# Moving the last two thirds of an adaLN modulation from VectorE to quarter-array matmuls on TensorE, in a one-core hybrid encoder layer

## The chip, the core and the metric

The kernel runs on one core of one Trainium2 chip. The metric is the device time of one execution in microseconds (us), the median of three runs. Engines are named as in the profile: PE is TensorE (PEld its weight loads), DVE is VectorE, ACT is ScalarE, POOL is GpSimd, SP is the queue from which all DMAs are issued.

## What is computed

One encoder layer over a prompt of 512 frames and a sample of 64 frames, all in float32. The change concerns the modulation vector `mod`: two conditioning vectors of 2048 elements (prompt and sample) pass through silu and a 2048 x 12288 matrix, and the result is cut into six shift, scale and gate vectors.

```
def trunk(x, c, states, params, block):
    ...
        mod = jax.nn.silu(c) @ w_ada[l] + b_ada[l]
        sh1, sc1, g1, sh2, sc2, g2 = jnp.split(mod[:, None, :], N_MOD, axis=-1)
        h = rmsnorm(x, norm1[l]) * (1 + sc1) + sh1
        mix, s_a, s_b, s_c = token_mixers(
        ...
        x = x + g1 * mix
        h = rmsnorm(x, norm2[l]) * (1 + sc2) + sh2
        f, s_f = conv_ffn(h, ffn_s[l], w_up[l], ffn_conv_w[l], ffn_conv_b[l], w_down[l])
        x = x + g2 * f
```

The mixers are a gated linear attention of 4 heads and a gated DeltaNet of 8 heads, evaluated in blocks of 64 or 128 frames between a wide input projection and an output projection. A convolutional FFN follows.

## The kernel before, in words

Large products run on PE as three float32r matmuls for each 128 x 128 weight tile and half of the frames (288 columns): high part times high part, high times low, low times high (`mm6`, L512 and L514). ACT and DVE split each weight tile into its parts ahead of time (`split`, L599 and L600).

**Stages.** `head` (to about 165 us of the span) norms the input and computes shift 1 and scale 1, that is columns 0 to 4095 of `w_ada`. The mixing stage (to about 1260 us) computes the input projection tile by tile and, woven into it, the recurrences. Then come the second half of the output projection, the FFN's upward products, and its downward products.

**The modulation in the head** (`modulation`, L659) goes by PE: for 512 columns and four k-tiles of 128 rows, four matmuls (L672) run, each with a stationary tile of 32 columns of which two hold the conditioning vectors (`cs`), each writing its own 32 partitions of one PSUM bank. The four quarters are summed at the end by a transposition on PE (L144) and a reduction on DVE (L678).

**The modulation in the mixing stage** (`ada_block`, L757) goes by DVE: columns 4096 to 12287, 16 blocks of 512. For each block, DVE multiplies each of 16 k-tiles (128 x 512) by a column of the conditioning vector and adds it to an accumulator, for both vectors: 32 instructions (L770 for the first k-tile, L772 for the others). Then eight PE matmuls of one column (L778) sum over the partitions, and DVE adds the bias (L747). The weights come in loads of two k-tiles, 512 KB each (L764), into a pool of two buffers with the tag `xr`; the same two buffers serve the reloads of the input in the output projection (`x_tile`, L1093) and some reloads of mixer outputs.

**What sets the order.** The mixing stage is one stream of `mm6` calls; after each (one k-tile, six matmuls) `tick` (L479) advances the recurrences' generators by one step and the modulation's generator by 0.65 steps. A `yield` ends a step, and `rest(n)` lets n steps pass with nothing. A scheduler then fixes the order of each engine's instructions before the program runs; every engine's queue, SP's too, is worked in that order.

**The inverse.** Each DeltaNet head needs the inverse of 16 x 16 triangular blocks (`inverse16`, L331). It goes: PE L216 (products of keys), DVE, a store by SP (L340) and four loads (L345), some 30 small steps on POOL (L347 to L354), a store (L355) and two loads (L358), and two DVE instructions (L362) that spread the result. There are nine of these: eight prompt heads, here h0 to h7, and the sample. While one head's inverse is on its way, the steps of the head before run on PE: L276, L283, L289, L301 to L305 four times over, then a norm (DVE L137, POOL L138, ACT) and a transposition on PE (L144).

Of the kernel before, what the change touches and what calls it, by code (L numbers as in the profile page):

```python
# [16 lines left out]
P = 128  # L17
# [78 lines left out]
class Kern:  # L96
# [510 lines left out]
    def head(self, pool):  # L607
# [8 lines left out]
        nc.gpsimd.memset(cs, 0.0)  # L616
        for s in range(2):
            A.activation(self.ct[:, s], self.vmap[f"c{s}"], AF.Silu)
            V.tensor_copy(cs[:, :, s], self.ct[:, s])
        self.mod = self.cp.tile([P, 6, KD, 2], F32, name="mod")  # L620


# [36 lines left out]
        def modulation(g):  # L659
            for mi in (1, 0):  # L660
                ps = self.bank()
                c0 = mi * D + g * 512
                for k0 in range(0, KD, 4):
                    yield
                    raws = [hraw().rearrange("p (k n) -> p k n", k=2) for _ in range(2)]
                    for n, raw in enumerate(raws):
                        k1 = k0 + 2 * n
                        nc.sync.dma_start(raw, i["w_ada"][0, k1 * P:(k1 + 2) * P, c0:c0 + 512].rearrange("(k p) n -> p k n", p=P))

                    for k in (2, 3, 0, 1):  # L670
                        with self.tc.issue_after(last) if k == 0 else nullcontext():
                            T.matmul(ps[32 * k:32 * k + 32], cs[:, k0 + k], raws[k // 2][:, k % 2], start=(k0 == 0), stop=(k0 == KD - 4))  # L672
                        last = nc.cur_bb.bb.instructions[-1]
                rw = pool.tile([P, 512], F32, tag="rw", bufs=1, name=self.name("rw"))
                V.tensor_copy(rw, ps)
                pc = self.transpose4(rw.rearrange("p (b t) -> p b t", b=4))
                m = pool.tile([P, 4, 2], F32, tag="msum", bufs=2, name=self.name("msum"))
                V.tensor_reduce(m, pc.rearrange("p b (j q) -> p b q j", j=4)[:, :, 0:2], axis=mybir.AxisListType.X, op=ALU.add)  # L678
# [12 lines left out]
        for g in range(4):  # L691
# [22 lines left out]
                next(mods, None)  # L714
            for _ in mods:
                pass

    def pair_w(self, offs, k0):

# [34 lines left out]
            out[:, k0:k0 + n], self.mod[:, mi, k0:k0 + n], 1.0,  # L754
            self.vec(norm, k0, n).unsqueeze(2).to_broadcast([P, n, 2]), op0=ALU.add, op1=ALU.mult)

    def ada_block(self, blk, acc, raw):  # L757

        nc = self.nc
        V, T = nc.vector, nc.tensor  # L760
        acc = [a() for a in acc]
        for k0 in range(0, KD, 2):
            w = raw().rearrange("p (k n) -> p k n", k=2)
            nc.sync.dma_start(w, self.i["w_ada"][0, k0 * P:(k0 + 2) * P, blk * 512:(blk + 1) * 512]  # L764
                              .rearrange("(k p) n -> p k n", p=P))
            for k in range(2):
                for s in range(2):
                    col = self.ct[:, s, k0 + k:k0 + k + 1]
                    if k0 + k == 0:
                        V.tensor_scalar_mul(acc[s], w[:, k], col)  # L770
                    else:
                        V.scalar_tensor_tensor(acc[s], w[:, k], col, acc[s], op0=ALU.mult, op1=ALU.add)  # L772
                    yield
        yield from self.rest(4)
        pc = self.bank()
        for j in range(4):
            for s in range(2):
                T.matmul(pc[:, 2 * j + s:2 * j + s + 1], acc[s][:, j * P:(j + 1) * P], self.c["ones"][:, 0:1],  # L778
                         start=True, stop=True)
        self.put_mod(blk // 4, 4 * (blk % 4), pc[:, :8].rearrange("p (j s) -> p j s", s=2))  # L780

    def ada_blocks(self, blocks, acc):
        for blk in blocks:
            yield from self.ada_block(blk, acc, self.xr)


    def w_in(self, off):
# [746 lines left out]
def layer_kernel(tc, i, o):  # L1534
    nc = tc.nc
    with ExitStack() as ctx:
# [16 lines left out]
        with ExitStack() as early:  # L1553
            K.wp = pool(early, "wp", "right", bufs=3)
            with ExitStack() as right:
# [9 lines left out]
                with ExitStack() as st:  # L1565
                    K.ap = pool(st, "ap", bufs=1)
                    K.jobs, K.at_job, K.at_ada = [], 0.0, 0.0
                    K.dp = dp
                    acc = [lambda n=n: K.ap.tile([P, 512], F32, tag=f"acc{n}", bufs=1, name=K.name("acc")) for n in range(2)]
# [12 lines left out]
                    for _ in K.ada:  # L1582
                        pass
# [101 lines left out]
```

## Time and profile before

| | |
|---|---|
| median of three runs | 2984.51 us (2979.99 to 2984.74) |
| the profiled execution | 2981.26 us, span 2979.5 us |
| mean granted TensorE clock | 0.980 |
| PE, DVE, ACT, POOL busy | 96%, 69%, 40%, 11% of the span |
| PE without work in 200 to 1260 us | 66 us |
| DVE in L772 | 480 instructions, 340.5 us |
| DVE in L770 | 32 instructions, 14.7 us |
| moved by DMA | 395.55 MB, mean 133 GB/s |

How to read the rows in the prediction: a row of the timeline has the start, the duration (of a run of like instructions, from the first start to the last end), the engine, the line of the program, the operation, out<-in, the count, and in brackets how long the engine was idle before and what ended the wait. PE's rows overlap, since matmuls are pipelined: what one costs in the stream is read from one start to the next. A float32 matmul shows as two records, a float32r matmul as one. A row of stretches has the length of the stretch, the busy time of each engine with its instruction count, the granted clock (1.00 is full speed), and the busy share and GB/s of the DMA engines.

### The profile page before, as it was taken

To read this page: it belongs to the slowest core of one execution; us is meant where nothing else is said; L and a number is where in the kernel's file an instruction comes from. 1 tells how busy PE (TensorE), PEld (TensorE's weight loads), DVE (VectorE), ACT (ScalarE), POOL (GpSimd) and SP (SyncE) were. 2 spreads that over 40 slices of the span, in tenths; PEclk is the share of its full clock that TensorE was granted. 3 is DMA by queue.
4 is the path that set the end of the run, shared out by engine and by line. 5 is a ranking of instruction groups with operands and counts; after the bars stand their busy time and mean duration, and the time that the engine had idled before them with its cause. 6 is when DMAs were issued, how large, how long until landed. Compare 5 with 4: busy or idle time off the path is not lost.

```text
span 2979.5 us, 52341 instructions
## 1 busy us (share of the span) xinstructions
PE 2863.4 (96%) x21060; PEld 2772.9 (93%) x21060; DVE 2050.0 (69%) x3234; ACT 1179.3 (40%) x2015; POOL 338.0 (11%) x609
## 2 busy tenths in 40 slices
PE   6998899999899999999999999999999999999998
PEld 3688888999889998999999999999999999999997
DVE  2366766667668867557888888888888865555555
ACT  4234444444445333245444444444444421222223
POOL 0004323333120000000011111111111100000000
PEclk8999999999999999999999999999999999999999
DMA  8864544444454446643333333333333473333221
GB/s 269 285 185 121 150 143 124 128 129 144 134 159 130 137 132 194 199 140 97 106 105 111 109 103 107 111 102 105 115 105 105 133 236 101 111 101 113 84 85 66
DMA packets 535446, 395.55 MB, mean 133 GB/s; under 512 B 59657, under 2 KB 465412, under 8 KB 535204
## 3 DMA queue, kind: packets, MB, share of 16 engines
q1 hardware_dynamic: 535204, 392.21, 44.0%
q8 instruction: 166, 2.72, 0.4%
q14 instruction: 76, 0.62, 0.1%
HBM read 356.47 MB, written 35.67 MB: 132 GB/s over the span
## 4 chain that ended last, share of the span: by engine, by line
PE 71%; DVE 3%; DMA 2%; POOL 1%; issue 1%; ACT 1%; SPq 0%; ACTq 0%; DVEq 0%; POOLq 0%
PE g L512 22%; PE bank L1301 11%; PE bank L1300 11%; PE bank L1302 11%; PE g L514 11%; DVE acc L772 1%; PE bank L405 1%; PE bank L144 1%; DMA xr<-in_w_ada_dram 1%; DMA xr<-in_x_prompt_dram 1%; PE bank L778 1%; DVE wl L600 0%; POOL m L352 0%; POOL m L351 0%; POOL s L138 0%
## 5 line engine op out<-in xcount | busy, mean ns | idle before, releaser
L1301 PE MATMUL bank<-slot,wh 128*128 128x290 f32 x2464 | 736.3, 299 | 0.0
L1300 PE MATMUL bank<-slot,wh 128*128 128x290 f32 x2464 | 734.0, 298 | 0.0
L1302 PE MATMUL bank<-slot,wl 128*128 128x290 f32 x2464 | 728.2, 296 | 0.0
L512 PE MATMUL g<-slot,wh 128*128 128x288 f32 x3168 | 551.7, 295 | 0.3 <-DVE slot L1070 0.3
L512 PE MATMUL g<-hh,wh 128*128 128x288 f32 x2048 | 473.1, 310 | 0.0
L1302 PEld LDWEIGHTS bank<-slot,wl 128*128 128x128 f32 x2464 | 470.8, 191 | 0.0
L1301 PEld LDWEIGHTS bank<-slot,wh 128*128 128x128 f32 x2464 | 469.8, 191 | 0.1
L512 PEld LDWEIGHTS g<-slot,wh 128*128 128x128 f32 x3168 | 465.8, 188 | 0.7 <-DVE slot L1070 0.5
L599 ACT ACTIVATE wh<-raw 128x1024 fp32r<-128x1024 f32 x215 | 227.5, 1059 | 601.9 <-PE g L512 572.1
L1300 PEld LDWEIGHTS bank<-slot,wh 128*128 128x128 f32 x2464 | 464.2, 188 | 0.1
L512 PE MATMUL g<-hl,wh 128*128 128x288 f32 x2048 | 461.6, 304 | 0.0
L514 PE MATMUL g<-hh,wl 128*128 128x288 f32 x2048 | 459.9, 303 | 1.6 <-DVE wl L600 1.6
L1070 DVE SCALAR_TENSOR_TENSOR slot<-g,mod,slot 128x512 f32<-128x512 f32 (+1 forms) x448 | 202.1, 492 | 284.2 <-PE g L514 283.2
L772 DVE SCALAR_TENSOR_TENSOR acc<-xr,ct,acc 128x512 f32<-128x512 f32 x480 | 340.5, 752 | 26.6 <-DMA xr<-in_w_ada_dram 26.0
L512 PEld LDWEIGHTS g<-hh,wh 128*128 128x128 f32 x2048 | 336.6, 193 | 12.1 <-issue 9.8
L514 PEld LDWEIGHTS g<-hh,wl 128*128 128x128 f32 x2048 | 338.6, 193 | 8.4 <-issue 5.9
L512 PEld LDWEIGHTS g<-hl,wh 128*128 128x128 f32 x2048 | 340.4, 193 | 4.4 <-issue 3.9
L514 PE MATMUL g<-slot,wl 128*128 128x288 f32 x1584 | 342.8, 295 | 0.0
L600 DVE TENSOR_TENSOR wl<-raw,wh 128x1024 fp32r<-128x1024 f32 x215 | 262.5, 1221 | 62.4 <-ACT wh L599 61.7
L1247 ACT ACTIVATE wh<-raw 128x1024 fp32r<-128x1024 f32 x176 | 186.0, 1057 | 221.9 <-PE bank L1301 185.6
L514 PEld LDWEIGHTS g<-slot,wl 128*128 128x128 f32 x1584 | 255.3, 188 | 0.0
L1248 DVE TENSOR_TENSOR wl<-raw,wh 128x1024 fp32r<-128x1024 f32 x176 | 215.4, 1224 | 54.3 <-ACT wh L1247 54.3
(354 smaller groups left out, 3160.9 us busy)
## 6 DMA issues: line engine op xcount, KB each, us to landing
raw<-in_w_up_dram SPq DMA_DIRECT2D x176, 512.0 KB
xr<-in_w_ada_dram SPq DMA_DIRECT2D x128, 512.0 KB
raw<-in_w_in_dram SPq DMA_DIRECT2D x100, 512.0 KB
raw<-in_w_down_dram SPq DMA_DIRECT2D x88, 512.0 KB
hraw<-in_w_ada_dram SPq DMA_DIRECT2D x64, 512.0 KB
raw<-in_w_out_dram SPq DMA_DIRECT2D x32, 512.0 KB
slot<-actd SPq DMA_DIRECT2D x44, 288.0 KB
actd<-v SPq DMA_DIRECT2D x44, 256.0 KB
```

Of the source, the lines that this page charges most:

```text
L144: self.nc.tensor.transpose(ps[:, b * P:(b + 1) * P], src4[:, b], self.c["ident"])
L512: T.matmul(ps[:, h if bank is None else bank, :n], wh, x[:, h, :n], start=f, stop=False)
L514: T.matmul(ps[:, h if bank is None else bank, :n], wl, ah[:, h, :n], start=False, stop=stop)
L599: nc.scalar.activation(hi[:, :n_], raw[:, :n_], AF.Copy)
L600: nc.vector.tensor_tensor(lo[:, :n_], raw[:, :n_], hi[:, :n_].bitcast(F32), op=ALU.subtract)
L772: V.scalar_tensor_tensor(acc[s], w[:, k], col, acc[s], op0=ALU.mult, op1=ALU.add)
L1070: self.nc.vector.scalar_tensor_tensor(x1[:, :, z], ps[:, :, c], gain[:, q:q + 1], x1[:, :, z], op0=ALU.mult, op1=ALU.add)
L1247: self.nc.scalar.activation(hi, src, AF.Copy)
L1248: self.nc.vector.tensor_tensor(lo, src, hi.bitcast(F32), op=ALU.subtract)
L1300: T.matmul(ps, wh[:, j], hi, start=(c < 3 and j == 0), stop=False, skip_group_check=True)
L1301: T.matmul(ps, wh[:, j], lo, start=False, stop=False, skip_group_check=True)
L1302: T.matmul(ps, wl[:, j], hi, start=False, stop=(j == NPAIR - 1), skip_group_check=True)
```

## The change

All 16 blocks of the mixing stage are now computed in the manner of the head, with one difference: each group of four matmuls is a sum of its own (start and stop both set), and DVE adds it from PSUM to one accumulator in SBUF. The head's code is moved into helpers that both places call (`c_columns`, `quad`, `load_ada`, `quad_sum`); what it issues stays the same.

```
-    def ada_block(self, blk, acc, raw):
...
-        acc = [a() for a in acc]
-        for k0 in range(0, KD, 2):
-            w = raw().rearrange("p (k n) -> p k n", k=2)
-            nc.sync.dma_start(w, self.i["w_ada"][0, k0 * P:(k0 + 2) * P, blk * 512:(blk + 1) * 512]
-                              .rearrange("(k p) n -> p k n", p=P))
-            for k in range(2):
-                for s in range(2):
-                    col = self.ct[:, s, k0 + k:k0 + k + 1]
-                    if k0 + k == 0:
-                        V.tensor_scalar_mul(acc[s], w[:, k], col)
-                    else:
-                        V.scalar_tensor_tensor(acc[s], w[:, k], col, acc[s], op0=ALU.mult, op1=ALU.add)
-                    yield
-        yield from self.rest(4)
-        pc = self.bank()
-        for j in range(4):
-            for s in range(2):
-                T.matmul(pc[:, 2 * j + s:2 * j + s + 1], acc[s][:, j * P:(j + 1) * P], self.c["ones"][:, 0:1],
-                         start=True, stop=True)
-        self.put_mod(blk // 4, 4 * (blk % 4), pc[:, :8].rearrange("p (j s) -> p j s", s=2))
+    def quad(self, ps, c, raws, start, stop):
+
+        for k in (2, 3, 0, 1):
+            with self.tc.issue_after(last) if k == 0 else nullcontext():
+                self.nc.tensor.matmul(ps[32 * k:32 * k + 32], c[:, k], raws[k // 2][:, k % 2], start=start, stop=stop)
+            last = self.nc.cur_bb.bb.instructions[-1]
+
+    def load_ada(self, raws, blk, k0):
+        raws = [r.rearrange("p (k n) -> p k n", k=2) for r in raws]
+        for n, r in enumerate(raws):
+            k1 = k0 + 2 * n
+            self.nc.sync.dma_start(r, self.i["w_ada"][0, k1 * P:(k1 + 2) * P, blk * 512:(blk + 1) * 512].rearrange("(k p) n -> p k n", p=P))
+        return raws
+
+    def quad_sum(self, rw, m):
+
+        pc = self.transpose4(rw.rearrange("p (b t) -> p b t", b=4))
+        self.nc.vector.tensor_reduce(m, pc.rearrange("p b (j q) -> p b q j", j=4)[:, :, 0:2], axis=mybir.AxisListType.X, op=ALU.add)
+
+    def ada_block(self, blk, acc):
+
+        V = self.nc.vector
+        acc = acc()
+        for k0 in range(0, KD, 4):
+            raws = self.load_ada([self.xr(), self.xr()], blk, k0)
+            yield from self.rest(6)
+            ps = self.bank()
+            self.quad(ps, self.c_col[:, k0:k0 + 4], raws, True, True)
+            if k0 == 0:
+                V.tensor_copy(acc, ps)
+            else:
+                V.tensor_tensor(acc, ps, acc, op=ALU.add)
+            yield from self.rest(2)
+        m = self.sp.tile([P, 4, 2], F32, tag="msum", bufs=2, name=self.name("msum"))
+        self.quad_sum(acc, m)
+        self.put_mod(blk // 4, 4 * (blk % 4), m)
```

A block had 36 steps of the generator (32 and a rest of 4); it has 32 (four times 6 and 2). In the program after, the quarter matmul is L757, the copy and the add from PSUM are L782 and L784, the reduction is L770, and the ada loads are still L764; the helper through which the recurrences record their instructions is L1633 (L1623 before).

**Place 1, PE, where a block of the modulation ends or a group of four k-tiles comes.** Before, eight one-column matmuls stood at the end of each block, 16 times in the stage (`g` is the projection's PSUM tile, `acc` the two accumulators):

```order
L514 MATMUL g_5346<-hh_896,wl_5349 128x288 x2
L778 MATMUL bank_5408<-consts_96,acc_4686 128x1
L778 MATMUL bank_5408<-consts_96,acc_4687 128x1
...
L778 MATMUL bank_5408<-consts_96,acc_4687 128x1
L512 MATMUL g_5346<-hh_915,wh_5348 128x288 x2
```

Now four quarter matmuls stand in the stream 64 times, the two of the second load ahead of the two of the first, and 16 times the four transpositions of a finished accumulator:

```order
L514 MATMUL g_3693<-hh_1517,wl_3784 128x288 x2
L757 MATMUL bank_3844<-xr_3763,c_col 32x512 x2
L757 MATMUL bank_3844<-xr_3762,c_col 32x512 x2
L512 MATMUL g_3693<-hh_1528,wh_3783 128x288 x2
...
L276 MATMUL bank_4381<-st_4369,qkv_3194 128x128
L144 MATMUL bank_4386<-consts_96,acc_3761 128x128 x4
```

The four quarter matmuls of a group stand together everywhere, with nothing between them; PE now reads the loaded weights itself.

**Place 2, DVE, around the two instructions that spread the inverse, at head h2's inverse** (`st` and `sq` are the state and the right side of the head before, which PE's L276 and L283 read). Before:

```order
L1623 SCALAR_TENSOR_TENSOR sq_3629<-bank_3628,kt_2428,m_3509 128x128
L772 SCALAR_TENSOR_TENSOR acc_3237<-xr_3828,ct,acc_3237 128x512
L600 TENSOR_TENSOR wl_3886<-raw_3884,wh_3885 128x1024
L1623 SCALAR_TENSOR_TENSOR st_3651<-st_3613,egl,bank_3649 128x128
L772 SCALAR_TENSOR_TENSOR acc_3238<-xr_3828,ct,acc_3238 128x512
L137 TENSOR_SCALAR s_540_3666<-s_539_3665 128x4
L362 TENSOR_TENSOR m_3901<-cm_3898,consts_1740 128x512
L362 TENSOR_TENSOR m_3902<-cm_3898,consts_1740 128x512
```

After:

```order
L784 TENSOR_TENSOR acc_3105<-bank_3560,acc_3105 128x512
L1633 SCALAR_TENSOR_TENSOR sq_3573<-bank_3572,kt_2424,m_3497 128x128
L362 TENSOR_TENSOR m_3893<-cm_3890,consts_1740 128x512
L362 TENSOR_TENSOR m_3894<-cm_3890,consts_1740 128x512
L1633 SCALAR_TENSOR_TENSOR st_3600<-st_3554,egl,bank_3598 128x128
L1633 SCALAR_TENSOR_TENSOR sq_3617<-bank_3616,kt_2424,m_3497 128x128
L1633 SCALAR_TENSOR_TENSOR st_3638<-st_3600,egl,bank_3636 128x128
L137 TENSOR_SCALAR s_553_3652<-s_552_3651 128x4
```

The accumulations are gone from between the recurrence's steps, and the two L362 now stand ahead of the last steps of the head before (three of them and the norm's first) where they stood behind them.

**Place 3, SP, at head h3's inverse.** Before, one ada load stood here and there among the others:

```order
L345 DMA m_4272<-d_609_4269 8x16x16 x4
L764 DMA xr_4688<-in_w_ada_dram 128x2x512
L900 DMA sd_v<-ts_4305 128x64
L598 DMA raw_4859<-in_w_in_dram 128x8x128
L764 DMA xr_4763<-in_w_ada_dram 128x2x512
L355 DMA d_610_4270<-m_4272 32x2x256
L358 DMA cm_4723<-d_610_4270 128x4x16 x2
```

After:

```order
L345 DMA m_4254<-d_627_4251 8x16x16 x4
L598 DMA raw_4752<-in_w_in_dram 128x8x128
L908 DMA sd_v<-ts_4285 128x64
L355 DMA d_628_4252<-m_4254 32x2x256
L598 DMA raw_4834<-in_w_in_dram 128x8x128
L764 DMA xr_4394<-in_w_ada_dram 128x2x512
L764 DMA xr_4395<-in_w_ada_dram 128x2x512
L358 DMA cm_4703<-d_628_4252 128x4x16 x2
```

The loads come in pairs, and here the pair stands behind the store that waits for POOL's steps.

More of the change, by code (lines that the diff above doesn't have):

```diff
@@ L661, in modulation @@
                 ps = self.bank()
-                c0 = mi * D + g * 512
                 for k0 in range(0, KD, 4):
                     yield
[L665 to L673, printed above, removed]
+                    raws = self.load_ada([hraw(), hraw()], mi * 4 + g, k0)
+                    self.quad(ps, cs[:, k0:k0 + 4], raws, k0 == 0, k0 == KD - 4)
                 rw = pool.tile([P, 512], F32, tag="rw", bufs=1, name=self.name("rw"))
                 V.tensor_copy(rw, ps)
-                pc = self.transpose4(rw.rearrange("p (b t) -> p b t", b=4))
                 m = pool.tile([P, 4, 2], F32, tag="msum", bufs=2, name=self.name("msum"))
-                V.tensor_reduce(m, pc.rearrange("p b (j q) -> p b q j", j=4)[:, :, 0:2], axis=mybir.AxisListType.X, op=ALU.add)
+                self.quad_sum(rw, m)
                 self.put_mod(mi, 4 * g, m)
@@ L716, in head, with c_columns @@
                 pass
+    def c_columns(self, cs):
+        self.nc.gpsimd.memset(cs, 0.0)
+        for s in range(2):
+            self.nc.vector.tensor_copy(cs[:, :, s], self.ct[:, s])
     def pair_w(self, offs, k0):
@@ L782, in ada_blocks @@
     def ada_blocks(self, blocks, acc):
         for blk in blocks:
[L784 removed]
+            yield from self.ada_block(blk, acc)
     def w_in(self, off):
```

9 lines of the change are left out of this document (4 added, 5 removed).

## The prediction

> **What bounds the kernel now.** I read the page's table of engines first, then the table of stretches for the mixing stage, then what PE waited for there, then the timeline around those waits.
>
> ```profile
> PE 2863.4 (96%) x21060; PEld 2772.9 (93%) x21060; DVE 2050.0 (69%) x3234; ACT 1179.3 (40%) x2015; POOL 338.0 (11%) x609
> ```
>
> PE is busy for 96% of the span; whatever is put on it lengthens the kernel, unless it falls into a gap. The change touches only the mixing stage, so its own row counts:
>
> ```profile
> 200.00:1260.00 1060.00, 993.93 (x7262) 954.69 (x7261) 731.99 (x1315) 456.55 (x1043) 214.48 (x433) 0.96 0.50 145
> ```
>
> PE has work for 993.93 of 1060 us here too, DVE (the third number) for 732. So PE bounds this stage as well, and at most 66 us of idle time plus what the clock loses (0.96 of full speed: about 4%, 42 us) could be won by relieving DVE. What PE waited for in that stretch:
>
> ```profile
> PE bank L144 <- ACT m L1623: 28.1, 10, 9.1
> PE bank L276 <- DVE st L1623: 8.7, 1, 8.7
> PE bank L778 <- DVE m L1623: 8.3, 1, 8.3
> PE bank L144 <- ACT qkv L924: 5.9, 4, 1.9
> PE bank L144 <- DMA xr<-in_x_prompt_dram: 3.3, 6, 0.9
> ```
>
> The first three rows are 45 us of the 66. They are few and long, about one for each DeltaNet head. One of them, at head h5, in order of time:
>
> ```profile
> 580.67 1.05 PE L216 MATMUL bank<-qkv 128*128 128x128 f32 x8
> ...
> 606.01 0.69 DVE L362 TENSOR_TENSOR m<-cm,consts 128x512 f32<-128x512 f32 x1 [4.07 <-DMA cm<-d]
> ...
> 607.95 0.16 DVE L137 TENSOR_SCALAR s<-s 128x4 f32<-128x4 f32 x1
> 608.20 1.18 POOL L138 TENSOR_TENSOR s<-s,mhalf 128x4 f32<-128x4 f32 x1 [5.99 <-DVE s L137]
> ...
> 609.86 0.47 PE L144 MATMUL bank<-consts,m 128*128 128x128 f32 x1 [2.36 <-ACT m L1623]
> ```
>
> The inverse leaves PE at L216 and is back at DVE's L362 25.3 us later (606.01 - 580.67). DVE works in order, so all that stands behind L362 waits: here the norm of the head before, then POOL, ACT, and PE's transposition. The long waits are thus not DVE's load but the inverse's round trip through SP and POOL, and the change leaves that in place. A wait costs more than its length, because the clock falls; the stretches right after the wait that ended at 313.6 us, and 8 us later:
>
> ```profile
> 314.00:318.00 4.00, 4.00 (x19) 3.98 (x18) 1.79 (x3) 2.44 (x5) 0.00 (x0) 0.50 0.54 166
> 322.00:326.00 4.00, 4.00 (x33) 4.00 (x32) 4.00 (x6) 1.95 (x4) 2.06 (x2) 1.00 0.45 132
> ```
>
> At half clock 19 matmuls start in 4 us, at full clock 33: some 6 us of half clock cost about 3 us for each long wait.
>
> **What the change adds to PE.** The head already runs such groups, between the same kind of matmuls:
>
> ```profile
> 83.91 0.30 PE L514 MATMUL g<-hh,wl 128*128 128x288 f32 x1
> 84.13 1.06 PE L672 MATMUL bank<-hraw,cs 128*32 128x512 f32 x8
> 85.13 0.41 PE L514 MATMUL g<-hh,wl 128*128 128x288 f32 x1
> 85.38 0.43 PE L512 MATMUL g<-hh,wh 128*128 128x288 f32 x2
> ```
>
> All eight records (four float32 matmuls) fit into 1.06 us, so the quarters do run side by side. From 83.91 to 85.38 are 1.47 us for two other matmuls, which without a group take 0.27 (two starts at 0.133 us, as in the stretches of pure projection). One group costs 1.20 us, and 64 groups **77 us**. [...]
>
> The four transpositions at the end of a block, from the head as well:
>
> ```profile
> 92.81 0.43 PE L512 MATMUL g<-hl,wh 128*128 128x288 f32 x2
> 93.08 0.60 PE L144 MATMUL bank<-consts,rw 128*128 128x128 f32 x4
> 93.44 0.51 PE L514 MATMUL g<-hh,wl 128*128 128x288 f32 x2
> 93.79 0.43 PE L512 MATMUL g<-hh,wh 128*128 128x288 f32 x2
> ```
>
> 0.98 us for four other matmuls that take 0.53: 0.45 us, 16 times, **7 us**.
>
> **What it removes from PE.** The sixteen records of L778:
>
> ```profile
> 603.68 1.84 PE L778 MATMUL bank<-consts,acc 128*128 128x1 f32 x16
> 605.39 0.51 PE L512 MATMUL g<-hh,wh 128*128 128x288 f32 x2
> ```
>
> 1.71 us, 16 times: **27 us** less. Net, PE has 57 us more to do, all of it in its own stream, where nothing hides it.
>
> **What it does to DVE.**
>
> ```profile
> L772 DVE SCALAR_TENSOR_TENSOR acc<-xr,ct,acc 128x512 f32<-128x512 f32 x480 | 340.5, 752 | 26.6 <-DMA xr<-in_w_ada_dram 26.0
> L770 DVE TENSOR_SCALAR acc<-xr,ct 128x512 f32<-128x512 f32 x32 | 14.7, 481 | 16.6 <-PE bank L778 16.6
> L1623 DVE TENSOR_TENSOR m<-bank,m 128x512 f32<-128x512 f32 x18 | 12.2, 686 | 4.0 <-ACT m L1623 4.0
> ```
>
> It loses 355 us and gains 64 additions or copies from PSUM at 0.69 us, 44 us: 311 us less. None of this is on the path by itself, since PE's waits for the weight splits and for most steps of the recurrences are small already. It matters in one place, the round trip of the inverse, because POOL's steps stretch while DVE accumulates. Two round trips (the POOL part only), all instructions first, then those on `acc` alone:
>
> ```profile
> 733.40:753.40 20.00, 18.65 (x139) 17.68 (x137) 15.20 (x24) 8.53 (x19) 16.29 (x34) 1.00 0.28 83
> 589.20:602.20 13.00, 12.83 (x89) 11.23 (x88) 5.58 (x10) 4.57 (x13) 9.54 (x32) 1.00 0.31 85
> ```
>
> ```profile
> 733.40:753.40 20.00, 0.00 (x0) 0.00 (x0) 9.75 (x14) 0.00 (x0) 1.00 0.28 83
> 589.20:602.20 13.00, 0.00 (x0) 0.00 (x0) 0.00 (x0) 0.00 (x0) 1.00 0.31 85
> ```
>
> With 14 accumulations beside it POOL's part took 20 us, with none 13. After the change every inverse should be near the 13, and near the 25.3 us from L216 to L362 that h5 shows. [...]
>
> **What of the waits stays.** I counted PE's work in the new order from each L216 to the first PE row that needs a DVE instruction behind L362, with the costs above. For h0, h1 and the sample it is 29, 48 and 38 us, more than the round trip: no wait, where before h0 and h1 waited 8.3 and 9.1. For h2 to h7 it is 20.1, 23.3, 23.7, 24.1, 20.7 and 20.5. Three of them need `st` of place 2, ready 27.3 us after L216 (25.3, two L362 at 0.7, 0.35 for the step, 0.25 to PE): 6.9 us of waiting each. Three need the norm, ready after 29.2 us (609.86 - 580.67): 5.5 each. That is 37 us; the same count on the order of before gives 12.8 us for h3 to h5, of whose three waits (4.9, 4.1, 2.4) the sum is 11.4, so I take nine tenths, 33 us. With 3 us of clock each, six waits cost 51 us after; seven long ones cost 45 + 21 = 66 us before. Gain: **15 us**.
>
> **Smaller terms.** The blocks now need 512 steps instead of 576, so the modulation ends before the output projection begins, and the two `xr` buffers are free there for the input: the 3.3 us of the last row of waits go, **3 us** gained. In exchange PE itself waits for the loads, where DVE did. A load's price:
>
> ```profile
> 753.84 0.38 SPq L764 DMA_DIRECT2D xr<-in_w_ada_dram  x1
> 757.97 1.42 DVE L772 SCALAR_TENSOR_TENSOR acc<-xr,ct,acc 128x512 f32<-128x512 f32 x2 [9.14 <-DMA xr<-in_w_ada_dram]
> ...
> 822.81 6.10 SPq L764 DMA_DIRECT2D xr<-in_w_ada_dram  x2
> 829.10 3.50 DVE L772 SCALAR_TENSOR_TENSOR acc<-xr,ct,acc 128x512 f32<-128x512 f32 x4 [0.58 <-DMA xr<-in_w_ada_dram]
> ```
>
> 4.1 us alone, 6.3 us with others on the way. A pair starts when the group before it has read its buffers: 1.2 us for the group, 0.8 for two issues, 6.3 to land, 8.3 us from group to group. In the new order the groups are 5.5 to 21 us of PE work apart; only two distances are below 8.3 (5.5 and 7.8), some 16 lie between 9.7 and 10.8. Pairs queued behind the inverse's store (place 3) are late when PE waits for that inverse anyway. I take **4 us**; below it nothing is to be gained, above it 1 us at each of 60 groups would be 60. What waits behind a group on PE is the whole projection, so this cost is paid in full.
>
> **The sum.** 77 + 7 - 27 - 15 - 3 + 4 = 43 us on the profiled execution's 2981.3 us (span 2979.5 and 1.8 around it): **3024 us**. That execution lies inside the three runs (2979.99 to 2984.74), so I set nothing between it and the median.
>
> **The rivals.**
> - *PE waits for its loads.* SP's order is fixed, and a store or a weight load that waits ahead of a pair delays the group and all of PE. For it: SP waits often, and over a quarter of the distances leave less than 2.5 us. Against it: DVE, on the same loads, waited only 26.0 us in all (row of L772). At 1 us per group, or a dozen waits of 4 to 5 us: 3024 + 60 = 3084.
> - *Relieved DVE wins: faster.* If the inverse came back within about 20 us of L216, all 66 us of those waits and their clock would go: 57 - 66 - 3 = -12, 2969 us. The point is 20 us, PE's work at h2, h6 and h7. Against it: the 25.3 us are already those of an inverse without accumulations beside it, and POOL's part is only 13 of them.
> - *The quarters don't run side by side here* and the change isn't what it says: four times 1.06 us, 3.2 us more for each group: 3024 + 64 x 3.2 = 3229 us. Against it stands the 1.06 us of the head, with tiles of the same shape.
>
> **How the numbers follow.** Forecast (3000 to 3050): 0.62. Waiting for loads (3050 to 3110): 0.20. Relieved DVE (2945 to 3000): 0.15, of which I put 0.09 below 2978 and 0.04 in the band around no change, 2978 to 2990. Serial quarters: 0.03. The range for 8 in 10 is 2988 to 3084. A measurement of this kernel can tell about 0.2%, 6 us, from no change. Faster 0.09, same 0.04, slower 0.87.
>
> **What would show it.** The groups: eight records of L757 within about 1.1 us, and some 75 us of PE's busy time on that line. The waits: L362 some 25 us after L216 for every head, PE idle for 4 to 7 us at six heads, near none at h0 and h1. POOL's part near 13 us everywhere. The loads: PE's waits for `xr` of a few us in all. The prediction is wrong if PE's waits for `xr` add up to tens of us, if the waits at h2 to h7 are gone, or if groups cost much more or less than 1.2 us.

## The result and the profile after

The changed kernel takes **3009.23 us** (median of 4 runs, 3006.11 to 3013.59) against 2984.62 us for the kernel before beside it (4 runs, 2979.99 to 2988.34): a ratio of **1.0084, 95% interval 1.0065 to 1.0104**, or 25 us slower (19 to 31). The forecast was 43 us slower. The profiled execution took 3007.98 us, span 3006.2, granted clock 0.986.

The row of engines on the page, the row of the mixing stage from the view of stretches (columns as in the prediction), and what PE waited for in that stretch:

```profile
PE 2902.9 (97%) x21380; PEld 2750.0 (91%) x21380; DVE 1770.3 (59%) x2804; ACT 1175.3 (39%) x2013; POOL 290.5 (10%) x610
```

```profile
200.00:1260.00 1060.00, 1006.42 (x7398) 907.27 (x7399) 445.93 (x876) 446.70 (x1029) 167.12 (x433) 0.98 0.48 143
```

```profile
PE bank L276 <- DVE st L1633: 17.8, 3, 7.0
PE bank L144 <- ACT m L1633: 14.1, 7, 5.9
PE bank L222 <- DVE msum L770: 6.2, 1, 6.2
PE bank L144 <- DMA xr<-in_x_prompt_dram: 4.6, 1, 4.6
```

DVE lost 280 us of work (2050.0 to 1770.3) and PE gained 40 (2863.4 to 2902.9). Idle time fell from 66 to 54 us in these 1060 us, and the clock rose from 0.96 to 0.98. The prediction had put 3 us on the clock; the table below has 13.5. It isn't the accident of one execution: over the whole span the granted clock was 0.984 to 0.986 in the four executions of the changed kernel, and 0.976 to 0.983 in 44 executions of the kernel before that ran beside the experiments.

The whole difference lies in the mixing stage. It begins at 209.8 us in both executions, and its last product ends, and the output projection begins, at 1290.9 before and at 1318.0 after: 27.1 us. What comes behind takes 1688.6 and 1688.1 us. I split the 27 us by PE's timeline, from the start of each row to the start of the next, without the wait that ended last:

| us in the stage | before | after | difference | forecast |
|---|---|---|---|---|
| groups of the modulation (L757) | 0 | 64.7 | +64.7 | +77 |
| one-column matmuls (L778) | 29.3 | 0 | -29.3 | -27 |
| transpositions of blocks' sums | 0 | 6.0 | +6.0 | +7 |
| projection (L512, L514) | 792.6 | 788.0 | -4.6 | |
| recurrences and all else | 194.2 | 197.5 | +3.3 | |
| PE idle | 65.0 | 52.0 | -13.0 | about -11 |
| of the rows above, lost to the half clock | 31.4 | 17.9 | -13.5 | -3 |

The last row is (1 - granted clock) times PE's busy time, summed over stretches of 2 us; it is contained in the rows above it, which is why the projection got shorter although groups now stand between its matmuls. The two rows of busy time, of after and of before:

```profile
209.82:1318.05 1108.23, 69.06 (x512) 10.16 (x512) 0.98 0.48 143
```

```profile
209.81:1290.88 1081.07, 31.44 (x256) 31.62 (x256) 0.96 0.51 146
```

A group in the timeline of after, between the same kind of rows as in the prediction:

```profile
402.88 0.43 PE L514 MATMUL g<-hh,wl 128*128 128x288 f32 x2
403.24 1.07 PE L757 MATMUL bank<-xr,c_col 128*32 128x512 f32 x8
404.23 0.53 PE L512 MATMUL g<-hh,wh 128*128 128x288 f32 x2
404.61 0.43 PE L512 MATMUL g<-hl,wh 128*128 128x288 f32 x2
```

1.07 us for eight records, and 404.61 - 402.88 = 1.73 us less four starts at 0.133: 1.20 us, as forecast. Over 34 such places the mean is 1.198.

### The profile page after: what moved, and what is told of

It reads as the page before. It is cut to its first block, busy times and chain, and to the rows that moved or that the text cites. A ratio compares the mean times of both kernels' runs of the same rounds, so it can differ in the third digit from the quotient of the medians.

```text
span 3006.2 us, 52540 instructions
## 1 busy us (share of the span) xinstructions
PE 2902.9 (97%) x21380; PEld 2750.0 (91%) x21380; DVE 1770.3 (59%) x2804; ACT 1175.3 (39%) x2013; POOL 290.5 (10%) x610
## 4 chain that ended last, share of the span: by engine, by line
PE 71%; issue 2%; DVE 1%; ACT 1%; DMA 1%; POOL 1%; ACTq 0%; SPq 0%; POOLq 0%; DVEq 0%
PE g L512 22%; PE bank L1309 11%; PE bank L1308 11%; PE g L514 11%; PE bank L1310 11%; PE bank L405 1%; PE bank L757 1%; PE bank L144 1%; PE bank L441 0%; PE bank L1518 0%; PE bank L447 0%; DVE m L1633 0%; PE bank L444 0%; ACT wh L599 0%; DMA raw<-in_w_out_dram 0%
## 5 line engine op out<-in xcount | busy, mean ns | idle before, releaser
L512 PE MATMUL g<-slot,wh 128*128 128x288 f32 x3168 | 551.7, 295 | 0.3 <-DVE slot L1078 0.3
L512 PE MATMUL g<-hh,wh 128*128 128x288 f32 x2048 | 474.3, 311 | 0.0
L512 PEld LDWEIGHTS g<-slot,wh 128*128 128x128 f32 x3168 | 465.8, 188 | 0.7 <-DVE slot L1078 0.5
L514 PE MATMUL g<-hh,wl 128*128 128x288 f32 x2048 | 453.9, 301 | 0.0
L512 PE MATMUL g<-hl,wh 128*128 128x288 f32 x2048 | 453.3, 300 | 0.0
L512 PEld LDWEIGHTS g<-hh,wh 128*128 128x128 f32 x2048 | 331.0, 191 | 56.5 <-issue 52.9
L514 PE MATMUL g<-slot,wl 128*128 128x288 f32 x1584 | 343.0, 295 | 0.0
L512 PEld LDWEIGHTS g<-hl,wh 128*128 128x128 f32 x2048 | 335.3, 191 | 6.0 <-issue 5.9
L514 PEld LDWEIGHTS g<-hh,wl 128*128 128x128 f32 x2048 | 334.7, 191 | 6.3 <-issue 6.0
L514 PEld LDWEIGHTS g<-slot,wl 128*128 128x128 f32 x1584 | 255.3, 188 | 0.0
L1255 ACT ACTIVATE wh<-s 128x1024 fp32r<-128x1024 f32 x132 | 140.2, 1062 | 208.8 <-DVE s L1266 106.8
```

The lines of the kernel that those rows point to most:

```text
L512: T.matmul(ps[:, h if bank is None else bank, :n], wh, x[:, h, :n], start=f, stop=False)
L514: T.matmul(ps[:, h if bank is None else bank, :n], wl, ah[:, h, :n], start=False, stop=stop)
L1255: self.nc.scalar.activation(hi, src, AF.Copy)
```

## The experiments

Two theories stood against each other after this reading. **W**, that of the prediction: PE's waits for the inverses lower the clock, VectorE's load sets those waits, so the clock's gain is VectorE's relief. **N**: a stretch of one-column matmuls lowers the clock by itself, so a part of the gain is L778's going. A third question was whether a group costs PE its full 1.2 us.

All runs in one table. "Stage" is the length of the mixing stage, "idle" and "clock" are the last two rows of the table above for each kernel, "beside" counts VectorE's multiply-adds of 128x512 that ran while one of the nine inverses was on POOL (from L340 to L355). Ratios are to the kernel before, on the same chip; a difference in us in the text is the ratio times 2984.6. Stage, idle, clock and beside are of the one profiled execution of each kernel. Of the idle time, 36.6 us in e8 and 10.8 us in e12 lie at the stage's end, behind the last block.

| kernel | median us | ratio (95%) | stage | idle | clock | beside |
|---|---|---|---|---|---|---|
| before | 2984.62 | 1 | 1081.1 | 65.0 | 31.4 | 68 |
| after | 3009.23 | 1.0084 (1.0065 to 1.0104) | 1108.2 | 52.0 | 17.9 | 0 |
| e1_groups_twice | 3067.81 | 1.0268 (1.0255 to 1.0282) | 1165.6 | 54.1 | 18.2 | 0 |
| e2_one_quarter | 3176.87 | 1.0630 (1.0615 to 1.0644) | 1271.9 | 56.2 | 19.3 | 0 |
| e3_transposes | 2973.90 | 0.9951 (0.9936 to 0.9966) | 1075.2 | 77.0 | 25.5 | 73 |
| e4_narrow_sums | 2977.26 | 0.9961 (0.9949 to 0.9972) | 1076.4 | 55.7 | 33.7 | 0 |
| e5_both | 3065.74 | 1.0259 (1.0245 to 1.0273) | 1160.5 | 89.3 | 33.6 | 83 |
| e6_no_ending | 2992.97 | 1.0010 (1.0001 to 1.0019) | 1086.1 | 105.5 | 22.9 | 129 |
| e7_endings_twice | 3029.32 | 1.0137 (1.0121 to 1.0153) | 1126.8 | 63.2 | 52.9 | 67 |
| e8_endings_split | 3053.03 | 1.0214 (1.0198 to 1.0231) | 1150.1 | 135.7 | 33.0 | 99 |
| e9_load_spread | 3070.72 | 1.0274 (1.0260 to 1.0288) | 1163.7 | 96.8 | 32.1 | 134 |
| e10_no_groups | 2944.37 | 0.9850 (0.9837 to 0.9864) | 1041.1 | 55.4 | 17.6 | 0 |
| e11_load_half | 3039.18 | 1.0191 (1.0173 to 1.0209) | 1133.6 | 78.8 | 18.2 | 77 |
| e12_two_rates | 3020.27 | 1.0123 (1.0108 to 1.0138) | 1116.5 | 114.6 | 31.8 | 109 |

### What a group costs

**e1: each group twice.**

```
-            self.quad(ps, self.c_col[:, k0:k0 + 4], raws, True, True)
+            self.quad(ps, self.c_col[:, k0:k0 + 4], raws, True, False)
+            self.quad(ps, self.c_col[:, k0:k0 + 4], raws, False, True)
```

> The changed kernel with each of the 64 groups issued twice into the same bank, so the modulation is doubled; loads and VectorE's work stay. [...] Rival H (part of a group lies in TensorE's waits and costs nothing): +20 us or less, at most 3030 us.

The ratio is 0.0184 above that of after, 55 us (48 to 62), and the stage is 57.4 us longer: 0.90 us for each further group, with idle time the same. Nothing of it is hidden in PE's waits; rival H falls. It is less than the 1.20 us that the forecast took for each group.

**e10: no groups at all.**

```
-            ps = self.bank()
-            self.quad(ps, self.c_col[:, k0:k0 + 4], raws, True, True)
             if k0 == 0:
-                V.tensor_copy(acc, ps)
+                V.tensor_tensor(acc, raws[0][:, 0], raws[1][:, 0], op=ALU.add)
             else:
-                V.tensor_tensor(acc, ps, acc, op=ALU.add)
+                V.tensor_tensor(acc, raws[0][:, 0], acc, op=ALU.add)
```

> The changed kernel without its 64 groups on TensorE: VectorE adds the first of each group's loaded tiles in their place (so the modulation is wrong); loads, steps, transpositions and VectorE's count of operations stay. With the kernel before it prices the two halves of the change: what TensorE pays, and what VectorE's relief and the going of the one-column matmuls give. If the 64 groups cost what the sum of the prediction took, 77 us: 3009 - 77 = 2932 us, and the gains are then 52 us. If a group costs what the second of a pair cost (3068 - 3009 = 59 us for 64): 2950 us, gains of 34 us. If the gains are only the sum of the two parts measured alone (15 us for the endings, 11 us for VectorE's sums on 8 columns): 2960 us.

Against after the ratio falls by 0.0234: the 64 groups cost **70 us** (63 to 77), 67.1 us in the stage, 1.05 to 1.09 us each. Part of the going of the groups was lost again to 3.4 us more idle time; PE's busy time in the stage differs by 70.5 us, 1.10 each. The forecast's 77 us is at the upper end. What makes up the last 0.1 us to the 1.20 read at 34 places isn't shown. A first group costs 1.05 to 1.10 us in the stage and a second one in a row 0.90 (e1); what makes up the 0.15 to 0.2 us between them, 10 to 13 us in all, isn't shown either. Against before, this kernel shows the other half of the change: **45 us gained** (41 to 49), where the forecast's terms were -27 + 7 - 15 - 3 = -38.

**e2: one quarter only.**

```
-            self.quad(ps, self.c_col[:, k0:k0 + 4], raws, True, True)
+            for k in range(4):
+                self.nc.tensor.matmul(ps[:32], self.c_col[:, k0 + k], raws[k // 2][:, k % 2], start=(k == 0), stop=(k == 3))
...
+                V.memset(acc, 0.0)
+                V.tensor_copy(acc[:32], ps[:32])
             else:
-                V.tensor_tensor(acc, ps, acc, op=ALU.add)
+                V.tensor_tensor(acc[:32], ps[:32], acc[:32], op=ALU.add)
```

> The changed kernel with the four matmuls of a group one behind the other on one quarter of the array, summed in the PSUM bank: the quarters taken away, the same sums. The prediction put four serial matmuls of 512 columns at 4.4 us against 1.20 us for the group, which is +205 us: 3209 to 3229 us. [...]

One group of e2, and one pair of e1:

```profile
418.40 0.43 PE L514 MATMUL g<-hh,wl 128*128 128x288 f32 x2
418.76 3.62 PE L781 MATMUL bank<-xr,c_col 128*32 128x512 f32 x8
422.31 0.54 PE L512 MATMUL g<-hh,wh 128*128 128x288 f32 x2
```

```profile
408.07 1.92 PE L757 MATMUL bank<-xr,c_col 128*32 128x512 f32 x16
```

3.62 us in place of 1.07: the stage is 164 us longer than that of after. The quarters do run side by side, and that rival is dead. Its price in the prediction was too high (four times 1.06 us; it is four times 0.9), and so was the range expected here, 3209 to 3229 us against 3177 measured.

### What lowers the clock

**e3: transpositions at the endings, nothing else changed.**

```
-        pc = self.bank()
-        for j in range(4):
-            for s in range(2):
-                T.matmul(pc[:, 2 * j + s:2 * j + s + 1], acc[s][:, j * P:(j + 1) * P], self.c["ones"][:, 0:1],
-                         start=True, stop=True)
-        self.put_mod(blk // 4, 4 * (blk % 4), pc[:, :8].rearrange("p (j s) -> p j s", s=2))
+        m = self.sp.tile([P, 4, 2], F32, tag="msum", bufs=2, name=self.name("msum"))
+        for s in range(2):
+            pc = self.transpose4(acc[s].rearrange("p (b t) -> p b t", b=4))
+            V.tensor_reduce(m[:, :, s], pc, axis=mybir.AxisListType.X, op=ALU.add)
+        self.put_mod(blk // 4, 4 * (blk % 4), m)
```

> The kernel before with one part of the change alone: a block's ending goes over transpositions in place of the one-column matmuls. The 128 one-column matmuls of 16 blocks (31.4 us busy at L778) are replaced by 128 transpositions of 128 columns, which at the changed kernel's 6.0 us for 64 are 12 us, and VectorE sums each of them. Theory N (the one-column matmuls lower the clock behind them, 6.7 us lost in the four stretches of the kernel before that follow an L778 block): -19 for the stream and -7 for the clock, 2955 to 2961 us, and no lowered stretch within 10 us behind a block's ending without a wait. Theory W (the clock is lowered by TensorE's waits alone, and the changed kernel's higher clock came from its shorter waits for VectorE): -19 alone, 2963 to 2968 us, and the 14 lowered stretches stay.

14.6 us faster than before (10 to 19): **faster than both kernels**, though by a little less than either theory said. In the profiled executions, whose spans differ by 7.6 us, the stage is 5.9 us shorter: endings 14.3 us in place of 29.3, the projection 5.9 us less with the clock's loss 5.9 us less, everything else 3 us more, and 12 us more idle time. No stretch is lowered without idle time ahead of it, as N says, where before had three; W's 14 stretches became 11.

**e6: no endings.**

```
-        pc = self.bank()
-        for j in range(4):
-            for s in range(2):
-                T.matmul(pc[:, 2 * j + s:2 * j + s + 1], acc[s][:, j * P:(j + 1) * P], self.c["ones"][:, 0:1],
-                         start=True, stop=True)
-        self.put_mod(blk // 4, 4 * (blk % 4), pc[:, :8].rearrange("p (j s) -> p j s", s=2))
+        self.put_mod(blk // 4, 4 * (blk % 4), acc[0][:, :8].rearrange("p (j s) -> p j s", s=2))
```

> The kernel before without the one-column matmuls: the sum over partitions is left out, the bias is added to the first eight columns of the accumulator, so the modulation is wrong. It prices L778 in all. By the sum of the prediction -27 us: 2957 us. Theory N (one-column matmuls lower the clock as well): -27 to -31 and -7 for the clock, 2946 to 2951 us, and fewer lowered stretches than the 14 of before. Theory W (waits alone lower the clock): 2954 to 2959 us, all 14 stretches still there.

All were missed: the kernel is as slow as before, 3 us slower (0 to 6). The stream lost its 29 us and the clock's loss fell to 22.9, but idle time rose by 40. The multiply-adds in two stretches of before and of e6 (length, VectorE's busy time on L772 with the count, clock, DMA) show why:

```profile
530.00:610.00 80.00, 22.83 (x33) 0.96 0.44 125
1050.00:1170.00 120.00, 30.46 (x44) 1.00 0.47 138
```

```profile
530.00:610.00 80.00, 37.57 (x52) 0.94 0.56 160
1050.00:1170.00 120.00, 0.00 (x0) 1.00 0.27 76
```

Without an ending on PE, which reads the accumulators, the blocks run ahead: 52 multiply-adds in the 80 us in place of 33, 434 of the 480 done by 900 us in place of 323, and 129 beside the inverses in place of 68. So e6 priced where VectorE's load stands as much as L778.

**e7: endings twice.**

```
-        for j in range(4):
+        for j in (0, 1, 2, 3, 0, 1, 2, 3):
             for s in range(2):
                 T.matmul(pc[:, 2 * j + s:2 * j + s + 1], acc[s][:, j * P:(j + 1) * P], self.c["ones"][:, 0:1],
```

> The kernel before with the one-column matmuls of each of the 16 endings issued twice into the same columns, nothing else changed. The second 16 x 8 of them cost the stream another 29 us (29.3 us for the first ones). Theory N (a stretch of one-column matmuls counts as idle for the clock, which was at 0.5 for 3.4 us behind three such endings without any wait): an ending is now 3.6 us long, longer than the 3.41 us grid on which the lowered stretches begin, so 10 to 16 more of them are followed by a lowered stretch of 1.7 us lost: 2985 + 29 + 17 to 27 = 3031 to 3041 us, and more than 10 lowered stretches with less than 0.5 us of idle ahead. Theory W (only TensorE's waits lower the clock): 3014 us, and no more than three or four such stretches.

41 us slower (36 to 46), of which the stage's clock loss is 21.5. First an ending of before that nothing interrupted, and the stretches around it; then one of e7:

```profile
1197.81 1.95 PE L778 MATMUL bank<-consts,acc 128*128 128x1 f32 x16
1199.62 0.38 PE L512 MATMUL g<-hl,wh 128*128 128x288 f32 x1
```

```profile
1196.86:1200.28 3.42, 3.42 (x29) 3.19 (x29) 0.49 (x3) 0.71 (x2) 0.00 (x0) 1.00 0.78 228
1200.28:1203.69 3.41, 3.41 (x16) 3.41 (x16) 1.80 (x4) 0.00 (x0) 0.00 (x0) 0.50 0.93 287
1203.69:1207.10 3.41, 3.41 (x28) 3.41 (x27) 2.01 (x4) 1.06 (x1) 0.00 (x0) 1.00 1.01 274
```

```profile
409.92 3.63 PE L778 MATMUL bank<-consts,acc 128*128 128x1 f32 x32
```

```profile
410.10:413.50 3.40, 3.40 (x32) 3.40 (x33) 0.67 (x2) 1.73 (x3) 0.31 (x2) 1.00 0.08 20
413.50:416.90 3.40, 3.40 (x16) 3.40 (x16) 3.40 (x8) 0.00 (x0) 0.00 (x0) 0.50 0.08 10
416.90:420.30 3.40, 3.40 (x27) 3.40 (x27) 3.29 (x6) 0.00 (x0) 0.00 (x0) 1.00 0.73 210
```

PE is busy for all of the first stretch, and the next 3.41 us run at half clock with half as many matmuls, 1.7 us lost. In e7 fourteen of the sixteen endings do this, in before three. That is what theory N says: half clock behind one-column matmuls, without any wait. It doesn't say that waits don't do it; most lowered stretches of every kernel but e7 stand behind them (11 of 14 in before, 10 of 13 in e4, 7 of 21 in e7).

**e8: endings in four pairs.**

```
         for j in range(4):
+            yield from self.rest(2 if j else 0)
             for s in range(2):
```

> The kernel before with the eight one-column matmuls of an ending issued in four pairs about 1.5 us or more apart, for 13 of the 16 blocks; the number of them is the same. Theory N (what counts is the share of a 3.41 us stretch that they fill): no lowered stretch without idle ahead behind a split ending, the three of the kernel before go, -5 us for the clock, 2977 to 2983 us. Theory W: no change, 2985 us, and three or so such stretches remain. The stream's 29 us stay by both.

No lowered stretch without idle time ahead remains, as N expects; the time was missed by both, 64 us slower (59 to 69), and the clock's loss as a whole did not fall (33.0): all its 12 lowered stretches stood behind waits, and those were longer (135.7 us idle against 65.0). Its two last endings tell where more than half of that went:

```profile
1325.19 3.71 PE L779 MATMUL bank<-consts,acc 128*128 128x1 f32 x16 [12.33 <-DVE acc L772]
1353.16 3.71 PE L779 MATMUL bank<-consts,acc 128*128 128x1 f32 x16 [24.26 <-DVE acc L772]
```

The six further rests in each of 16 blocks are 96 steps; the last two blocks were not done when the stage's products were, and PE waited 36.6 us for them. The modulation's pace has no room to spare.

### What VectorE's load costs

**e4: multiply-adds on 8 of 512 columns.**

```
-                        V.scalar_tensor_tensor(acc[s], w[:, k], col, acc[s], op0=ALU.mult, op1=ALU.add)
+                        V.scalar_tensor_tensor(acc[s][:, :8], w[:, k, :8], col, acc[s][:, :8], op0=ALU.mult, op1=ALU.add)
```

> The kernel before with VectorE's 512 multiply-adds on 8 of the 512 columns only, the rest of the modulation left out: VectorE's relief alone, without a group on TensorE and with the one-column matmuls left in place. Theory W (VectorE's load sets the waits on the inverses and with them the clock): the waits fall from 45 to about 30 us and the loss by the clock from 31 to about 18, -28 us, 2957 us. Theory N (the clock's loss is in part the one-column matmuls'): the waits fall by 13 to 15 us and the clock's loss by 5 to 7, -20 us, 2962 to 2967 us, with lowered stretches still behind L778 near 600, 800, 1200 and 1250 us. If VectorE's load is worth nothing: 2984 us.

12 us faster (8 to 15), less than both theories said. Idle time fell by 9, but the clock's loss stayed (33.7), with three lowered stretches behind an ending without idle time. VectorE's relief alone didn't raise the clock, in any of the five executions (0.979 to 0.980 over the span): against W.

**e5: the multiply-adds put back as dead work**, eight behind each group, from the group's tiles.

```
+            for k in range(4):
+                for s in range(2):
+                    V.scalar_tensor_tensor(old, raws[k // 2][:, k % 2], self.ct[:, s, k0 + k:k0 + k + 1], old, op0=ALU.mult, op1=ALU.add)
```

> The changed kernel with VectorE's 512 multiply-adds of before put back as dead work: 8 behind each group, from the same loaded tiles into one accumulator that nobody reads. It prices VectorE's relief from the changed kernel's side. Theory W of the prediction (the relief shortens the waits on the inverses and with them the clock's loss): idle +13 us, clock +4 to +13 us, 3026 to 3035 us. If the clock's gain was the one-column matmuls going: idle +9 to +13 us, clock +0 to +4, 3018 to 3026 us. If the relief is worth nothing: 3009 us.

52 us above after (45 to 59), more than any expectation: idle +37, clock +16.

**e9: the same load, one in each step, from a constant.**

```
-            yield from self.rest(6)
+            for n in range(6):
+                self.dead(old, n, k0)
+                yield
...
-            yield from self.rest(2)
+            for n in range(6, 8):
+                self.dead(old, n, k0)
+                yield
...
+    def dead(self, old, n, k0):
+        self.nc.vector.scalar_tensor_tensor(old, self.c_col.rearrange("p k n -> p (k n)"), self.ct[:, n % 2, k0 + n // 2:k0 + n // 2 + 1], old,
+                                            op0=ALU.mult, op1=ALU.add)
```

> The changed kernel with 512 multiply-adds of 128x512 on VectorE as dead work, one in each step of the modulation as in the kernel before, from a constant that lies in SBUF, so that no load and no buffer waits for them (in the run with eight behind each group they came in a burst of some 6 us). Theory W (the relief is worth what the profiles of before and after differ by in idle time and a part of the clock): +13 to +25 us, 3022 to 3034 us. If it is worth only what the narrow sums gave on the kernel before: +5 to +11 us, 3014 to 3020 us. If the 57 us of the run with bursts were the load and not its place: 3050 us or more.

57 us above after (50 to 64): not the bursts, the load. POOL's steps of the inverse (the two groups of L351 and L352, idle time last), first of after, then of e9:

```profile
L351 POOL TENSOR_TENSOR m<-m 32x14 f32<-32x14 f32 (+6 forms) x126 | 45.0, 357 | 8.9
L352 POOL TENSOR_TENSOR m<-m 32x14 f32<-32x14 f32 (+6 forms) x126 | 40.6, 322 | 9.7
```

```profile
L351 POOL TENSOR_TENSOR m<-m 32x14 f32<-32x14 f32 (+6 forms) x126 | 58.8, 467 | 8.9
L352 POOL TENSOR_TENSOR m<-m 32x14 f32<-32x14 f32 (+6 forms) x126 | 58.5, 465 | 9.6
```

86 us became 117; from L340 to L355 the nine inverses take 205 us in e9, 166 in after, 189 in before.

**e11: half of e9's load** (`dead` returns where n is odd).

> The changed kernel with half of the dead multiply-adds of the run with the spread load: 256 in place of 512, in every second step. TensorE's idle time between 210 and 900 us against VectorE's busy time there was so far: 266 us 41, 287 50, 435 52, 455 56, 467 65, 486 73, 527 94, 549 78. Theory K (a knee near 450 us: up to there the chain of a head waits little for VectorE, beyond it each further operation is waited for): VectorE comes to about 405 us there, idle +5 to +10, clock +0 to +5, 3014 to 3024 us. Theory L (the wait grows evenly with the load): half of 61 us, 3034 to 3044 us.

32 us above after (24 to 40), about half of e9, as theory L has it: theory K, a knee, falls. VectorE's busy time from 210 to 900 us is 435 us here and in e7; PE's idle time there is 68 us here and 52 in e7, so that load alone doesn't set it. The half load wasn't spread evenly, though: the scheduler put 77 beside the first six inverses and none beside the last three. The 77 raised idle time by 27 us, the 134 of e9 by 45: about a third of a microsecond for each operation of 0.75 us.

**e12: e3 with another pace**, 0.60 in the heads and 0.75 behind them.

> The kernel before with transpositions at the endings, the fastest so far at 0.995 of before, with the modulation's pace at 0.60 in the heads and 0.75 in the projections behind them, in place of 0.65 throughout. Theory K: VectorE's busy time in the heads falls from 467 to about 437 us, below the knee: idle -8 to -12 us, 2960 to 2968 us. Rival: the last blocks come late, since VectorE was 76% busy behind the heads already, and TensorE waits for their sums at the stage's end: +5 to +30 us, 2980 to 3005 us.

37 us slower than before (32 to 41), more than both sides said. The rival has a part in it: the last block's ending came at the very end of the stage, in e3 36 us ahead of it, and PE then waited 10.8 us, not for the block's sum but for the first weights of the output projection's second half, whose load came late behind it:

```profile
1315.13 1.03 PE L144 MATMUL bank<-consts,acc 128*128 128x128 f32 x8
1326.96 1.33 PE L512 MATMUL g<-slot,wh 128*128 128x288 f32 x4 [10.79 <-ACT wh L599]
```

Theory K is plainly missed: VectorE's busy time from 210 to 900 us did fall (467 to 431 us), but 109 multiply-adds came to stand beside inverses in place of 73, and idle time rose from 77 to 104, without the wait at the end. Where the operations stand counts, and the pace moves that in ways that its value doesn't tell.

## Why the prediction was right, and where it was off

- **PE pays for what is put on it**: right, and it decides the sign. Groups 77 forecast, 67 to 70 measured by leaving them out, so this term was 7 to 10 us too high; transpositions 7, measured 6.0; L778 27, measured 29.3. 1.20 us from start to start at 34 places was right as a reading and about 0.1 us too much as a price.
- **The waits on the inverses**: right in size. For h2 to h7 the sum was to be 33 us, and is 29.9 (7.0, 6.0, 2.9, 3.3, 5.7, 5.0). The three waits for `st` and the three for the norm stand at the heads forecast. For h2 to h7 L362 comes 25.5 to 28.6 us after L216, where the forecast had 25.3, and POOL's part of the nine inverses takes 11.0 to 13.2 us, where it had 13; so the rival in which relieved VectorE wins had no ground. Seven of the nine had one of VectorE's copies or additions from PSUM (0.69 us) beside them and took 11.0 to 13.2 us, the two without 12.6 and 13.0; that these would cost POOL nothing was the author's estimate. The forecast said 25 us for every head: it is 38 and 44 us at h0 and h1, whose first store (L340) is issued 10 and 22 us after L216, and 32 us for the sample. Unforeseen was a wait at h0, where the bank that PE needs at L222 is freed by a reduction that stands behind L362 on VectorE:

```profile
257.34 1.29 DVE L362 TENSOR_TENSOR m<-cm,consts 128x512 f32<-128x512 f32 x2 [8.17 <-DMA cm<-d]
258.55 0.18 DVE L770 TENSOR_REDUCE msum<-bank 128x8 f32<-128x32 f32 x1
258.79 2.08 PE L222 MATMUL bank<-qkv,qkv 128*128 128x128 f32 x8 [6.22 <-DVE msum L770]
```

- **The clock in the term "Gain: 15 us"**: this is the term furthest off. It took one long wait fewer at 3 us; measured are 13.5, 31.4 us in 14 lowered stretches against 17.9 in 8. The step that was missing: the prediction had the clock fall behind waits alone, but three of the 14, 5.1 us, stood behind one-column endings without any wait (in e7 14 of 16 endings did this, in e8, with the endings split, none). The other 8 us are fewer stretches behind waits, 8 in place of 11, of about the same length. e3 and e10 bound them from outside: with endings gone and VectorE's load kept the loss is 25.5, with both gone 17.6 (one profiled execution each), so the relief seems to have raised the clock there, and in e4, with the endings kept, it did not. How the two work together isn't settled.
- **x-tiles and loads**: PE waited 0.8 us for the modulation's loads where 4 was taken, and the rival in which PE waits for its loads didn't occur. But the 3.3 us of waits for the input weren't saved: one of 4.6 us remains, and two lowered steps of the clock behind it cost 2.8 us more. The modulation was done by then, as forecast (its last reduction is at 1188 us), but the load stood in SP's order behind a store that had waited 3.4 us for ACT, and the prediction had looked at the buffers alone:

```profile
1199.53 0.34 SPq L908 DMA_DIRECT2D sd_ar<-ts  x1
1199.97 1.60 SPq L1101 DMA_DIRECT2D xr<-in_x_prompt_dram  x1
1203.90 1.11 PE L144 MATMUL bank<-consts,xr 128*128 128x128 f32 x4 [4.57 <-DMA xr<-in_x_prompt_dram]
```

- **"The long waits are thus not DVE's load"** was half right: after the change the waits at h2 to h7 stay, but e5, e6, e9 and e11 show that multiply-adds beside an inverse lengthen them, by 0.3 to 0.4 us each (idle time above e10's 55 us, by the count beside the inverses). The kernel before got away cheaply: 68 of them, and 13 us more idle time than after. In e3, with 73, it is 25 us more. Why 68 cost so little there stays open.

The two halves as measured in the stage: 67.1 for the groups (e10 to after), less 40.0 for everything else (before to e10), which by construction is the 27.1 us. The forecast had 77 and 34, so both halves were off in the same direction, and its 43 us is 16 above what the stage shows; the sign and the main price were no luck.

## What to carry to other kernels

Where one engine is busy 95% of a stage, count what a change puts on it at full price, and look for the gain in what the same change removes from it: here the endings alone (e3, 0.9951 of before) were worth taking, and the groups cost more than VectorE's relief gave back. A busy matmul engine wasn't enough for its clock here: in e7 14 of 16 blocks of one-column matmuls were followed by a step of 3.41 us at 100% busy and 0.50, 1.7 us lost in it. Such rows are a cost to look for. When a change moves work on an engine off the critical path, compare where its instructions stand beside the round trips that are waited for, not its total load.

## What the runs showed of the hardware

- **The lowered stretches lie on a grid of 3.41 us.** All lowered stretches of one execution begin a multiple of that apart (in before 268.44 and 1200.28: 273 times 3.413), each is one or more steps long, at 0.50. I sorted the steps at full clock of the mixing stage, in all 14 profiles, by PE's idle time in them: with 2.2 us or more, all 105 were followed by a lowered step; with 1.8 to 2.2, 17 of 20; with 1.4 to 1.8, 17 of 50; with 1.0 to 1.4, 5 of 63; with 0.5 to 1.0, none of 168. By these counts it mattered whether 2 us of idle time lay in one step (17 of 20) or 1 us in each of two (5 of 63 or none). A lowered stretch had one to five steps, but for sixteen in a row around the two last waits of e8 (12.33 and 24.26 us); a step cost 1.7 us where PE had work. In these two steps of after 2.86 us of idle time lie in one step, and the next is lowered:

```profile
533.58:537.00 3.42, 0.56 (x4) 0.36 (x3) 1.95 (x5) 0.94 (x4) 1.01 (x1) 1.00 0.29 68
537.00:540.40 3.40, 3.40 (x15) 3.30 (x15) 0.69 (x1) 3.01 (x8) 0.00 (x0) 0.50 0.79 287
```

- **Lowered steps without idle time stood behind one-column matmuls.** With less than 0.5 us of idle time, 20 of 3876 steps were followed by a lowered one: all 20 in before, e4 and e7, the kernels with unbroken one-column endings, and none in the others. It went by how much of the step they filled: with 2.05 us or more of it, all 14 such steps were followed by a lowered one, with 1.8 to 2.05 us 6 of 15, with less none. For idle time the like counts, above, were all 105 from 2.2 us up and 17 of 20 from 1.8 to 2.2.
- A second group of four quarter matmuls in a row costs 0.90 us (e1), the first among full-array matmuls 1.05 to 1.10 (e10); four on one quarter take 3.62 (e2).
